# The first pair of ff tiles of a SwiGLU FFN as plain block products, with the sums of the seven-product scheme made behind them

## Chip, cores and metric

One Trainium2 chip, one core. The metric is device time of the whole program in microseconds (us), the median over runs of the same kernel. All data is float32. An operand of TensorE is a pair of reduced-precision float32 tiles, hi and lo (h is the rounded value, l what is left of it), and every product of two operands takes three matmuls: h·h, h·l and l·h.

## What is computed

Two layers over 640 tokens (128 of a prompt, 512 latent tokens), D = 1024. Layer 0 mixes tokens by attention and a state-space scan, layer 1 by a pooling mixer; each ends in a SwiGLU FFN with 22 ff tiles of 128. The part that the change touches is this:

```python
def swiglu(h, w_gate, w_up, w_down):
    return (jax.nn.silu(h @ w_gate) * (h @ w_up)) @ w_down

for l in range(DEPTH):
    ...                      # mix: MLA + SSD (layer 0), pool mixer (layer 1)
    xp = xp + g_p * rmsnorm(mix_p, norm_post_mix[l])
    xs = xs + g_s * rmsnorm(mix_s, norm_post_mix[l])
    fp = swiglu(modulate(xp, norm_pre_ffn[l], shf_p, scf_p), ffn_w_gate[l], ffn_w_up[l], ffn_w_down[l])
    fs = swiglu(modulate(xs, norm_pre_ffn[l], shf_s, scf_s), ffn_w_gate[l], ffn_w_up[l], ffn_w_down[l])
    xp = xp + gf_p * rmsnorm(fp, norm_post_ffn[l])
    xs = xs + gf_s * rmsnorm(fs, norm_post_ffn[l])
```

## The kernel before

**Tiles and halves.** Five token tiles of 128 hold the activations. For gate and up the 640 tokens are two halves of 320 (`HB`): half 0 is tokens 0 to 319, half 1 tokens 320 to 639. D is eight chunks of 128, four in each half of D. `prenorm` (L309 to L339) norms a token tile (square sum L315, root L104, reciprocal L105, scale L318 or L320 into `junk`), transposes it on TensorE (L328) into PSUM, and ACT (L335) and DVE (L333) evict it into `full`. The residual that is normed comes from L362, on DVE. Then `Halves.take(tt)` splits it.

**Seven products instead of eight.** The 22 ff tiles of gate and up are taken as 11 pairs. A `Matrix` is one pair of gate or of up, a 2 x 2 block matrix (ff tile x half of D), and so are the activations (half of D x half of the tokens). The four result blocks come from seven block products instead of eight, with sums of blocks on both sides; each product is 12 matmuls of 128x320 (four chunks, three each), at L497. So a pair needs 84 matmuls for each matrix, where plain products need 96. On the weight side `adds` (L467 to L470, POOL) makes the sums `q` and `t4` and overwrites a part of `rb`; `a`, `c`, `b` and `d` split raw weights or sums into hi (ACT, L89) and lo (L90, DVE unless another engine is named). On the activation side, `a1` holds the plain half 0, and `a2` five blocks on the columns of half 1: S2, S1, S3, S4 (sums) and A22 (plain). Products 1 and 2 use `a1` only; 6, 5, 7, 4 and 3 use `a2`.

**Where the sums are made.** For tiles 0 to 2 `take` splits into `a1` (DVE, L419 and L420). For tiles 3 and 4 it calls `pair`: three adds on DVE (L433, L435, L436), one on POOL (L434), into the tile `st`, then the splits into `a2h` (ACT, L410) and `a2l` (L411; DVE for the sums, POOL for A22).

**The order.** A scheduler of the framework sets the order of each engine's queue from the program's order, and each engine works through its queue in order. At an FFN's start, the first two tails (transposes and `take` of tiles 3 and 4) run among products 1 and 2 of the first gate g0 and the first up u0. Then, in the loop, product 6 and those after it follow. `p1`, `p2` and so on (L528 to L561) issue a product and what follows it: copies and adds of PSUM parts into `sg`, silu on ACT (L523), the gate's product with up on DVE (L526). `out_split` (L564 to L569) splits the gated tile into ah (ACT, L567) and al (POOL, L568); `down_add` multiplies it with w_down (L97 to L99, through `mm3`) and adds into `y` (L590), one pair later, in the slots `d()` between products. Raw weights come through a ring of four DMA buffers (`raw`), so a load waits until the work on an earlier one is done.

Of the kernel before, what the change touches and what calls it, by code (L numbers as in the profile page):

```python
# [9 lines left out]
F32 = mybir.dt.float32  # L10
# [7 lines left out]
P = 128  # L18
# [372 lines left out]
class Halves:  # L391
# [21 lines left out]
    def take(self, tt):  # L413
        nc = self.net.nc
        if tt < 3:
            cs = slice(tt * P, min(tt * P + P, HB))
            h, l = (a[:, :, cs] for a in self.a1)
            x = self.f[:, :, cs]
            nc.vector.tensor_copy(h, x)  # L419
            nc.vector.tensor_tensor(l, x, h.bitcast(F32), ALU.subtract)  # L420
        if tt == 3:
            self.pair(0, 64)
        if tt >= 3:
            self.pair(tt * P - HB, P)

    def pair(self, c0, n):
        nc = self.net.nc
        cs = slice(c0, c0 + n)
        fa, fb = self.f[:, :, cs], self.f[:, :, HB + c0 : HB + c0 + n]
        t = self.tmp.tile([P, 4, 4, P], F32, tag="st", name=self.net.name("st"))[:, :, :, 0:n]  # L430
        h, l = self.a2
        s1, s2 = t[:, self.S1], t[:, self.S2]
        nc.vector.tensor_tensor(s1, fb[:, 0:4], fb[:, 4:8], ALU.add)  # L433
        nc.gpsimd.tensor_tensor(t[:, self.S3], fa[:, 0:4], fb[:, 0:4], ALU.subtract)  # L434
        nc.vector.tensor_tensor(s2, s1, fa[:, 0:4], ALU.subtract)  # L435
        nc.vector.tensor_tensor(t[:, self.S4], fa[:, 4:8], s2, ALU.subtract)  # L436
# [63 lines left out]
def _ffn(net, l, A, fr, sp, tails, switch, finish):  # L500
# [112 lines left out]
    seq = [m for p in range(NPAIR) for m in mats(p)]
    seq[0], seq[1] = g0, u0
    prev = None
    wdn = None
    last = {}
    for n, m in enumerate(seq):
        p, up = divmod(n, 2)
        w = (wg, wu)[n] if n < 2 else Work(m, wg if up else None)  # L620
        if not up:
            wg = w
        nx = seq[n + 1] if n + 1 < len(seq) else None
# [3 lines left out]
        fill = [] if prev is None or final else list(range(NT))  # L627
# [16 lines left out]
        if nx and n != 0:  # L644
            nx.a()
# [13 lines left out]
        if up:  # L659
            at.append(out_split(wg, 1))  # L660
# [667 lines left out]
def trunk(ctx: ExitStack, tc: tile.TileContext, t: dict, o: dict):  # L1328
# [125 lines left out]
    A = Halves(net, ctx.enter_context(pool("a1", "right")))  # L1454

# [285 lines left out]
```

## Time and profile before

| | |
|---|---|
| median of 3 runs | 1479.79 us (1478.52 to 1483.55) |
| profiled execution | 1481.71 us |
| its span in the trace | 1479.9 us, mean granted clock 0.966 |
| PE busy | 1353.1 us, 91% |
| DVE busy | 1041.8 us, 70% |
| ACT busy | 662.5 us, 45% |
| POOL busy | 479.5 us, 32% |
| DMA | 164.38 MB, mean 111 GB/s |

PE is TensorE (its matmuls), DVE VectorE, ACT ScalarE, POOL GpSimd. A row of the timeline is: start in us from the start of the span, us that the work took, engine, line, operation, out<-in, shape, count, and in brackets the idle time of the engine just ahead of it with what ended that. Matmuls overlap, so the cost of one is the distance between two starts and not its own duration. [...]

### The profile page before, as it was taken

What the parts mean: (1) busy time and instruction counts of PE and PEld (TensorE: products, weight loads), DVE (VectorE), ACT (ScalarE), POOL (GpSimd) and SP (SyncE); (2) the same over time, 40 slices, a digit from 0 to 9 for tenths busy, and PEclk for the clock granted to TensorE, in tenths of its full rate; (3) what the DMA queues carried; (4) which work ended last, traced back from release to release, by engine and by line L of the source; (5) the groups of instructions that cost most, each with busy time, mean ns of one, the idle gap of its engine ahead of it and who ended that gap; (6) DMA issues with size and microseconds to landing.
All of it is one profiled execution on the core that took longest, in us unless ns stands there. A gap on an engine that the chain in (4) does not pass through costs nothing. (4 is left out here: it accounts for less than half of the span.)

```text
span 1479.9 us, 20167 instructions
## 1 busy us (share of the span) xinstructions
PE 1353.1 (91%) x7728; PEld 1152.2 (78%) x7728; DVE 1041.8 (70%) x1502; ACT 662.5 (45%) x1173; POOL 479.5 (32%) x385
## 2 busy tenths in 40 slices
PE   5999999999997599999999999855899999999997
PEld 2788764667576489898989998644789899999996
DVE  3755547787737777979876666898678766666656
ACT  3545645744225544343334334578353333433443
POOL 0000044244303553444253333322452533333320
PEclk8999999999998799999999999978899999999999
DMA  9434345500163232433332223221232332222213
GB/s 364 132 123 131 128 153 191 187 29 1 44 222 106 65 114 86 137 106 115 121 129 86 85 86 110 104 71 71 89 122 90 114 115 86 85 86 78 80 58 142
DMA packets 49988, 164.38 MB, mean 111 GB/s; under 512 B 6034, under 2 KB 9618, under 8 KB 49892
## 3 DMA queue, kind: packets, MB, share of 16 engines
q1 hardware_dynamic: 43056, 153.96, 31.4%
q10 hardware_dynamic: 6836, 9.14, 2.0%
q8 instruction: 60, 0.98, 0.3%
q14 instruction: 36, 0.29, 0.1%
HBM read 154.52 MB, written 8.56 MB: 110 GB/s over the span
## 5 line engine op out<-in xcount | busy, mean ns | idle before, releaser
L467 POOL TENSOR_TENSOR q<-raw,raw 128x512 f32<-128x512 f32 x44 | 62.8, 1427 | 451.5 <-DVE lc L90 225.8
L99 PE MATMUL ps<-hw,al 128*128 128x512 f32 x380 | 150.3, 396 | 4.4 <-POOL al L568 4.4
L590 DVE TENSOR_TENSOR y<-y,ps 128x512 f32<-128x512 f32 x180 | 120.5, 680 | 47.0 <-PE ps L99 46.3
L98 PE MATMUL ps<-lw,ah 128*128 128x512 f32 x380 | 150.4, 396 | 1.2 <-DVE lw L90 1.2
L97 PE MATMUL ps<-hw,ah 128*128 128x512 f32 x380 | 150.7, 396 | 0.0
L497 PE MATMUL ps<-a2h,hc 128*128 128x320 f32 x352 | 112.2, 320 | 38.0 <-ACT a2h L410 28.6
L497 PE MATMUL ps<-a2l,hc 128*128 128x320 f32 x352 | 112.0, 318 | 2.6 <-DVE a2l L411 2.6
L497 PE MATMUL ps<-a2h,lc 128*128 128x320 f32 x352 | 111.8, 319 | 0.0
L568 POOL TENSOR_TENSOR al<-sg,ah 128x640 fp32r<-128x640 f32 x44 | 82.4, 1877 | 90.8 <-ACT ah L567 69.4
L497 PE MATMUL ps<-a2h,lb 128*128 128x320 f32 x352 | 109.3, 311 | 0.0
L497 PE MATMUL ps<-a1h,ha 128*128 128x320 f32 x336 | 104.9, 312 | 4.9 <-DVE a1h L419 4.9
L497 PE MATMUL ps<-a2h,hb 128*128 128x320 f32 x352 | 109.0, 310 | 0.0
L497 PE MATMUL ps<-a2l,hb 128*128 128x320 f32 x352 | 108.8, 309 | 0.0
L497 PE MATMUL ps<-a1l,ha 128*128 128x320 f32 x336 | 104.5, 311 | 2.6 <-DVE a1l L420 2.6
L497 PE MATMUL ps<-a1h,la 128*128 128x320 f32 x336 | 104.3, 310 | 0.0
L497 PEld LDWEIGHTS ps<-a2h,hc 128*128 128x128 f32 x352 | 68.7, 196 | 41.3 <-ACT a2h L410 29.1
L90 DVE TENSOR_TENSOR lc<-q,hc 128x1024 fp32r<-128x1024 f32 x42 | 53.0, 1261 | 67.1 <-ACT hc L89 67.1
L99 PEld LDWEIGHTS ps<-hw,al 128*128 128x128 f32 x380 | 72.0, 190 | 23.4 <-POOL al L568 7.0
L89 ACT ACTIVATE hc<-q 128x1024 fp32r<-128x1024 f32 x44 | 46.6, 1059 | 94.6 <-PE ps L497 81.8
L98 PEld LDWEIGHTS ps<-lw,ah 128*128 128x128 f32 x380 | 72.2, 190 | 11.7 <-DVE lw L90 1.5
L97 PEld LDWEIGHTS ps<-hw,ah 128*128 128x128 f32 x380 | 72.1, 190 | 10.2
L89 ACT ACTIVATE hb<-raw 128x1024 fp32r<-128x1024 f32 x46 | 48.7, 1059 | 63.7 <-PE ps L497 31.6
(393 smaller groups left out, 3932.9 us busy)
## 6 DMA issues: line engine op xcount, KB each, us to landing
raw<-in_w_mod SPq DMA_DIRECT2D x80, 512.0 KB
raw<-in_w_gate SPq DMA_DIRECT2D x44, 512.0 KB
raw<-in_w_up SPq DMA_DIRECT2D x44, 512.0 KB
raw<-in_w_down SPq DMA_DIRECT2D x44, 512.0 KB
mraw<-in_w_mod SPq DMA_DIRECT2D x16, 512.0 KB
xs<-xd SPq DMA_DIRECT2D x10, 512.0 KB
x<-in_x_sample SPq DMA_DIRECT2D x8, 512.0 KB
raw<-in_w_xbc SPq DMA_DIRECT2D x8, 512.0 KB
```

The source lines that it names most:

```text
L89: self.nc.scalar.activation(h, x, AF.Copy)
L90: (eng or self.nc.vector).tensor_tensor(l, x, h.bitcast(F32), ALU.subtract)
L97: mm(out, ah, bh, start=first and i == 0, stop=False)
L98: mm(out, ah, bl, start=False, stop=False)
L99: mm(out, al, bh, start=False, stop=last and i == n - 1)
L467: g.tensor_tensor(self.q[:, lo], self.rb[:, lo], self.ra[:, lo], ALU.subtract)
L497: mm(out, x[:, k], z[:, k], start=first and n == 0, stop=n == len(terms) - 1, skip_group_check=True)
L568: nc.gpsimd.tensor_tensor(al, g.s[:, f], ah.bitcast(F32), ALU.subtract)
L590: nc.vector.tensor_tensor(yd, yd, out, ALU.add)
```

## The change

For the first pair of each FFN, gate and up are computed by plain block products. `plain(m, f, half)` makes one result block, 128 ff x 320 tokens, from eight chunks, so 24 matmuls through `mm3` (L97 to L99); silu reads PSUM, and the multiplication with up reads PSUM too (L626 and L628 of the kernel after). Half 1 needs plain activations: `take` now splits tiles 3 and 4 plainly, lower half of D into the slot S4 of `a2`, upper half into A22. The sums S1, S2 and S3 are made by `pair` behind the first half-1 product in the program; S4, whose slot is in use, is put into a spare part of `y` and split later by `fourth`. The weights of the first pair are split without sums, all four lo parts on POOL. `out_split` of the first pair is issued earlier, `gates` ahead of the loop, and the last pair's second al goes to DVE. PE's queue has 7011 rows instead of 6963.

```diff
@@ class Halves @@
+    def spare(self, y):
+        self.s4 = y.rearrange("p t d -> p (t d)")[:, NT * D - 4 * HB :].rearrange("p (k c) -> p k c", k=4)
+
+    def fourth(self):
+        h, l = self.a2
+        self.split(h[:, self.S4], l[:, self.S4], self.s4, self.net.nc.vector)
...
     def take(self, tt):
...
-        if tt == 3:
-            self.pair(0, 64)
-        if tt >= 3:
-            self.pair(tt * P - HB, P)
+        for c0, n in ((0, 64),) * (tt == 3) + ((tt * P - HB, P),) * (tt >= 3):
+            cs = slice(c0, c0 + n)
+            fb = self.f[:, :, HB + c0 : HB + c0 + n]
+            h, l = self.a2
+            for i, k in ((self.S4, 0), (self.A22, 4)):
+                self.split(h[:, i, :, cs], l[:, i, :, cs], fb[:, k : k + 4], nc.vector)
 
     def pair(self, c0, n):
...
-        nc.vector.tensor_tensor(t[:, self.S4], fa[:, 4:8], s2, ALU.subtract)
-        for i in range(2):
-            b = slice(2 * i, 2 * i + 2)
+        nc.vector.tensor_tensor(self.s4[:, :, cs], fa[:, 4:8], s2, ALU.subtract)
+        for b in (slice(0, 2), slice(2, 3)):
             self.split(
...
-        self.split(h[:, self.A22, :, cs], l[:, self.A22, :, cs], fb[:, 4:8], nc.gpsimd)
+
+    def plain(self, half):
+        if half == 0:
+            return [tuple(x[:, k] for x in self.a1) for k in range(KC)]
+        return [tuple(x[:, i, k] for x in self.a2) for i in (self.S4, self.A22) for k in range(4)]
@@ _ffn @@
-    def out_split(g, f):
+    def out_split(g, f, eng=None):
...
-        nc.gpsimd.tensor_tensor(al, g.s[:, f], ah.bitcast(F32), ALU.subtract)
+        (eng or nc.gpsimd).tensor_tensor(al, g.s[:, f], ah.bitcast(F32), ALU.subtract)
...
     g0, u0 = mats(0)
-    u0.tag_a = "w"
     g0.load()
     u0.load()
-    for m in (g0, u0):
-        m.a(nc.gpsimd)
-    g0.adds()
-    g0.c(nc.gpsimd)
-    wg = Work(g0)
-    wu = Work(u0, wg)
-    wg.p1()
+    w0 = {}
+    for f in range(2):
+        for m, tags in ((g0, "ab"), (u0, "cw")):
+            w0[m, f] = net.split(fr, tags[f], (m.ra, m.rb)[f], nc.gpsimd)
+    s0 = sp.tile([P, 2, TOK], F32, tag="sg", name=net.name("sg"))
+
+    def plain(m, f, half):
+        out = net.pt([P, HB])
+        wh, wl = (x.rearrange("p (k n) -> p k n", k=KC) for x in w0[m, f])
+        net.mm3(out, [(wh[:, k], wl[:, k], bh, bl) for k, (bh, bl) in enumerate(A.plain(half))])
+        d = s0[:, f, half * HB : half * HB + HB]
+        if m is g0:
+            nc.scalar.activation(d, out, AF.Silu)
+        else:
+            nc.vector.tensor_tensor(d, d, out, ALU.mult)
+
+    plain(g0, 0, 0)
     tails.pop(0)()
-    wg.p2()
-    wu.p1()
+    plain(u0, 0, 0)
     tails.pop(0)()
-    wu.p2()
+    plain(g0, 1, 0)
+    plain(u0, 1, 0)
+    plain(g0, 0, 1)
+    A.pair(0, 64)
+    A.pair(64, P)
+    plain(u0, 0, 1)
+    A.pair(192, P)
     switch(env)
     net.mrp = env["mac"]
-    g0.b()
-    g0.d()
...
+    seq = [m for p in range(1, NPAIR) for m in mats(p)]
+    n1 = seq[0]
+    n1.load()
+    at0 = [out_split(Out(s0), 0)]
+    n1.a()
+    n1.adds()
+    plain(g0, 1, 1)
+    n1.c()
+    plain(u0, 1, 1)
+    at0.append(out_split(Out(s0), 1))
+    n1.b()
+    n1.d()
+    A.fourth()
...
-            at.append(out_split(wg, 1))
+            at.append(out_split(wg, 1, nc.vector if final else None))
```

The order of the instructions shows what became of this. PE at the end of half 0 of the first FFN, before (`ps` is a PSUM tile, hw and lw the parts of u0's first operand, hc and lc those of the sum q of g0):

```order
L497 MATMUL ps_4604<-a1h,hw_4476 128x320
L497 MATMUL ps_4604<-a1l,hw_4476 128x320
L497 MATMUL ps_4604<-a1h,lw_4477 128x320
L497 MATMUL ps_4492<-a2h_4462,hc_4486 128x320
L497 MATMUL ps_4649<-a2h_4462,hc_4486 128x320
L497 MATMUL ps_4492<-a2l_4463,hc_4486 128x320
```

And after, at the same place (hw and lw are here the second ff tile of u0, ha and la the first of g0):

```order
L97 MATMUL ps_4615<-a1h,hw_4484 128x320
L98 MATMUL ps_4615<-a1l,hw_4484 128x320
L99 MATMUL ps_4615<-a1h,lw_4485 128x320
L97 MATMUL ps_4641<-a2h_4462,ha_4472 128x320
L98 MATMUL ps_4641<-a2l_4463,ha_4472 128x320
L99 MATMUL ps_4641<-a2h_4462,la_4473 128x320
```

The first matmuls on `a2` read sums S2 and S1 before, and plain activations in slot S4 after.

POOL at the start of the first FFN, before:

```order
L467 TENSOR_TENSOR q_4480<-raw_4466,raw_4464 128x512
L468 TENSOR_TENSOR q_4480<-raw_4466,q_4480 128x512
L469 TENSOR_TENSOR raw_4466<-raw_4466 128x512
L470 TENSOR_TENSOR t_891_4481<-raw_4464,q_4480 128x512
L90 TENSOR_TENSOR la_4473<-raw_4464,ha_4472 128x1024
L90 TENSOR_TENSOR lw_4477<-raw_4468,hw_4476 128x1024
L90 TENSOR_TENSOR lc_4487<-q_4480,hc_4486 128x1024
L411 TENSOR_TENSOR a2l_4463<-full_3857,a2h_4462 128x4x64
```

And after, where lines 446 and 482 to 485 are what lines 434 and 467 to 470 were:

```order
L90 TENSOR_TENSOR la_4473<-raw_4464,ha_4472 128x1024
L90 TENSOR_TENSOR lc_4477<-raw_4468,hc_4476 128x1024
L90 TENSOR_TENSOR lb_4481<-raw_4466,hb_4480 128x1024
L90 TENSOR_TENSOR lw_4485<-raw_4470,hw_4484 128x1024
L446 TENSOR_TENSOR st_4667<-full_3857 128x4x64
L482 TENSOR_TENSOR q_4741<-raw_4731,raw_4729 128x512
L483 TENSOR_TENSOR q_4741<-raw_4731,q_4741 128x512
L484 TENSOR_TENSOR raw_4731<-raw_4731 128x512
L485 TENSOR_TENSOR t_915_4742<-raw_4729,q_4741 128x512
```

The four adds ahead of la are gone, four weight splits stand in a row, and the next adds are those of the second gate.

ACT at the start of the second FFN, before (`sd` is the root of a square sum, of the table for square roots; `dump` is a square sum of the mix's output):

```order
L104 ACTIVATE sd_9098<-ss_1652_9090 128x1
L318 ACTIVATE junk_9051<-xs_8389,r_9055 128x1024
L531 ACTIVATE sg_9155<-ps_9157 128x320
L315 ACTIVATE junk_9105,ss_9106<-xs_8389 128x1024
L335 ACTIVATE full_8730<-ps_9171,mv_1571,mv_1572 128x128
L104 ACTIVATE sd_9108<-ss_9106,eps 128x1
L335 ACTIVATE full_8730<-ps_9171,mv_1571,mv_1572 128x128
L318 ACTIVATE junk_9105<-xs_8389,r_9109 128x1024
```

And after:

```order
L104 ACTIVATE sd_9093<-ss_1641_9085 128x1
L626 ACT_TABLE_LOAD
L626 ACTIVATE sg_9148<-ps_9149 128x320
L315 ACTIVATE junk_9100,ss_9101<-xs_8384 128x1024
L335 ACTIVATE full_8725<-ps_9175,mv_1571,mv_1572 128x128
L104 ACT_TABLE_LOAD
L104 ACTIVATE sd_9103<-ss_9101,eps 128x1
L335 ACTIVATE full_8725<-ps_9175,mv_1571,mv_1572 128x128 x2
L318 ACTIVATE junk_9100<-xs_8384,r_9104 128x1024
```

Where a copy stood (L531), silu stands, with a table load ahead of it and one ahead of the root that follows; a third load follows later, where before the only one was.

## Rows read from the trace of the kernel before

**Rows 1.** PE's waits, whole span: who waited for whom, us in total, times, longest.

```profile
PE ps L497 <- ACT a2h L410: 28.6, 2, 16.2
PE ps L497 <- DVE a2l L411: 2.6, 2, 2.3
```

**Rows 2.** Timeline of PE in the first FFN.

```profile
476.14 0.48 PE L328 MATMUL ps<-cm,junk 128*128 128x128 f32 x1 [2.19 <-DVE junk L320]
...
478.96 0.64 PE L497 MATMUL ps<-a1l,ha 128*128 128x320 f32 x1 [2.34 <-DVE a1l L420]
...
488.20 1.09 PE L328 MATMUL ps<-cm,junk 128*128 128x128 f32 x8 [0.84 <-DVE junk L320]
...
490.60 0.31 PE L497 MATMUL ps<-a1l,hw 128*128 128x320 f32 x1
490.75 0.31 PE L497 MATMUL ps<-a1h,lw 128*128 128x320 f32 x1
507.25 0.90 PE L497 MATMUL ps<-a2h,hc 128*128 128x320 f32 x2 [16.19 <-ACT a2h L410]
...
511.08 0.33 PE L497 MATMUL ps<-a2l,hc 128*128 128x320 f32 x1
```

**Rows 3.** Timeline of PE in the second FFN.

```profile
1016.24 0.33 PE L328 MATMUL ps<-cm,junk 128*128 128x128 f32 x1 [0.53 <-ACT junk L318]
...
1023.18 0.31 PE L497 MATMUL ps<-a1h,lw 128*128 128x320 f32 x1
1035.91 0.90 PE L497 MATMUL ps<-a2h,hc 128*128 128x320 f32 x2 [12.42 <-ACT a2h L410]
1039.10 0.63 PE L497 MATMUL ps<-a2l,hc 128*128 128x320 f32 x1 [2.29 <-DVE a2l L411]
1039.53 0.47 PE L497 MATMUL ps<-a2h,lc 128*128 128x320 f32 x1
...
1043.53 0.34 PE L497 MATMUL ps<-a2h,hc 128*128 128x320 f32 x1
...
1069.49 0.50 PE L99 MATMUL ps<-hw,al 128*128 128x512 f32 x1 [1.52 <-POOL al L568]
```

**Rows 4.** Windows: PE, PEld, DVE, ACT, POOL busy (x), PEclk, DMA share, GB/s.

```profile
500.00:510.00 10.00, 2.39 (x7) 1.99 (x8) 9.09 (x9) 3.06 (x3) 2.12 (x2) 0.50 0.18 52
```

**Rows 5.** Timeline of ACT and DVE in the first FFN's gap.

```profile
506.14 2.00 ACT L410 ACTIVATE a2h<-st 128x1024 fp32r<-128x1024 f32 x2 [4.68 <-DVE st L435]
...
500.23 1.21 DVE L411 TENSOR_TENSOR a2l<-st,a2h 128x1024 fp32r<-128x1024 f32 x1
```

**Rows 6.** Timeline of POOL and DVE at the first FFN's start.

```profile
473.02 2.51 POOL L90 TENSOR_TENSOR la<-raw,ha 128x1024 fp32r<-128x1024 f32 x1
475.48 2.88 POOL L90 TENSOR_TENSOR lw<-raw,hw 128x1024 fp32r<-128x1024 f32 x1
...
473.22 2.86 DVE L320 TENSOR_SCALAR junk<-x,r 128x1024 f32<-128x1024 f32 x1
476.01 2.90 DVE L420 TENSOR_TENSOR a1l<-full,a1h 128x512 fp32r<-128x512 f32 x1
```

**Rows 7.** Timeline of DVE and POOL in the pool mix.

```profile
959.30 4.95 DVE L362 SCALAR_TENSOR_TENSOR xs<-junk,r,xs 128x512 f32<-128x512 f32 x2
...
981.76 1.41 DVE L362 SCALAR_TENSOR_TENSOR xs<-junk,r,xs 128x512 f32<-128x512 f32 x2
...
985.21 1.78 POOL L467 TENSOR_TENSOR q<-raw,raw 128x512 f32<-128x512 f32 x1 [13.79 <-DMA raw<-in_w_up]
```

**Rows 8.** Timeline of ACT at its table load in the second FFN.

```profile
1023.79 1.28 ACT L523 ACT_TABLE_LOAD   x1
1025.08 0.47 ACT L523 ACTIVATE sg<-sg 128x320 f32<-128x320 f32 x1
```

**Rows 9.** Timeline of PE among the last products of the second FFN.

```profile
1448.86 0.50 PE L99 MATMUL ps<-ha,al 128*128 128x512 f32 x1 [0.80 <-POOL al L568]
```

More of the change, by code (lines that the diff above doesn't have):

```diff
@@ L429, in pair @@
         fa, fb = self.f[:, :, cs], self.f[:, :, HB + c0 : HB + c0 + n]
-        t = self.tmp.tile([P, 4, 4, P], F32, tag="st", name=self.net.name("st"))[:, :, :, 0:n]
+        t = self.tmp.tile([P, 3, 4, P], F32, tag="st", name=self.net.name("st"))[:, :, :, 0:n]
         h, l = self.a2
@@ L562, in p3, with __init__ @@
                 nc.vector.tensor_tensor(self.g.s[:, 1], self.g.s[:, 1], self.s[:, 1], ALU.mult)
-    def out_split(g, f):
+    class Out:
+        def __init__(self, s):
+            self.s = s
+    def out_split(g, f, eng=None):
         ah = env["at"].tile([P, TOK], F32R, tag="ah", name=net.name("ah"))
@@ L592, in _ffn @@
     g0, u0 = mats(0)
-    u0.tag_a = "w"
     g0.load()
     u0.load()
-    for m in (g0, u0):
-        m.a(nc.gpsimd)
-    g0.adds()
-    g0.c(nc.gpsimd)
-    wg = Work(g0)
-    wu = Work(u0, wg)
-    wg.p1()
+    w0 = {}
[13 more added lines that the diff above has]
+    plain(g0, 0, 0)
     tails.pop(0)()
-    wg.p2()
-    wu.p1()
+    plain(u0, 0, 0)
     tails.pop(0)()
-    wu.p2()
+    plain(g0, 1, 0)
[5 more added lines that the diff above has]
+    A.pair(192, P)
     switch(env)
     net.mrp = env["mac"]
-    g0.b()
-    g0.d()
[L613 to L616, printed above, removed]
+    seq = [m for p in range(1, NPAIR) for m in mats(p)]
[11 more added lines that the diff above has]
+    A.fourth()
+    prev = at0
+    wdn = net.split(fr, "w", down_load(0, 0), None)
+    env["gates"]()
     last = {}
-    for n, m in enumerate(seq):
+    for n, m in enumerate(seq, 2):
         p, up = divmod(n, 2)
-        w = (wg, wu)[n] if n < 2 else Work(m, wg if up else None)
+        w = Work(m, wg if up else None)
         if not up:
             wg = w
-        nx = seq[n + 1] if n + 1 < len(seq) else None
+        nx = seq[n - 1] if n - 1 < len(seq) else None
         final = p == NPAIR - 1
@@ L626, in _ffn @@
             last[0, 0] = net.split(fr, "w", down_load(NPAIR - 2, 0), None)
-        fill = [] if prev is None or final else list(range(NT))
+        fill = [] if final else list(range(NT))
         def d():
@@ L632, in d @@
             net.bg()
-        if nx and n != 0:
+        if nx:
             nx.load()
-        if n >= 2:
-            w.p1()
-            w.p2()
+        w.p1()
+        w.p2()
         if final and up:
@@ L643, in _ffn @@
         w.p5()
-        if nx and n != 0:
+        if nx:
             nx.a()
@@ L670, in _ffn @@
             prev = at
-        if nx and 1 <= n and (n + 1) // 2 < NPAIR - 1:
+        if nx and (n + 1) // 2 < NPAIR - 1:
             wdn = net.split(fr, "w", down_load((n + 1) // 2 - 1, (n + 1) % 2), None)
-        if n == 1:
-            env["gates"]()
     net.bg_drain()
@@ L1454, in trunk @@
     A = Halves(net, ctx.enter_context(pool("a1", "right")))
+    A.spare(y)
     def work_pools():
```

## The prediction

> **What bounds the kernel now.** The profiled execution took 1481.7 us over a span of 1479.9 us; the median of the three runs is 1479.8 us, so the profile lies 1.9 us above it. I make the sum as a difference and take it from both. A change of under 0.3% (4.4 us) is what a measurement of this kernel can't tell from none.
>
> I read the page first: TensorE (PE) is busy for 91% of the span, no other engine for more than 70%. So time comes back where PE waits, or where it does fewer matmuls. The list of what PE waits for shows where: the largest entry by far is two waits at L497 for a2h, 28.6 us together, one in each FFN; a2l adds 2.6 us to them [rows 1]. The timeline of PE gives each its place. In the first FFN half 0 ends with the matmul at 490.75, and the first matmul on a second-half operand starts at 507.25, after 16.19 us [rows 2]. In the second FFN the same gap is 12.42 us, with 2.29 us more for a2l [rows 3]. [...] What DVE and ScalarE (ACT) do there is build five blocks for tokens 320 to 639 from the last token tile and split each into hi and lo.
>
> **What the change removes.** The first pair of ff tiles no longer needs the sums. Half 1 of it reads the plain second-half activations, which `take` splits as soon as a tile's transposes are evicted. After the change the first matmul of half 1 needs a 128x512 split of the last tile, not three adds and two 128x1024 splits behind them. Does a matmul wait for its own block or for all of tile a2h? In the row of ACT at 506.14 two ACTIVATEs to a2h fill 2.00 us, to 508.14 [rows 5], while PE had started at 507.25 [rows 2]: the wait is for the block. So the sums can follow behind.
>
> Is PE busy long enough until they are there? Half 1 is now 4 x 24 = 96 matmuls, and products 1 and 2 of the next gate, which need only half 0, are 24 more. The spacing of full-clock matmuls is 0.147 us (0.15 from 490.60 to 490.75 [rows 2]), so they take 17.6 us. Tile 4 is transposed ahead of the last two plain products of half 0, another 7.1 us, from which I take 2 off for evicting it. DVE's queue from the last tile's split to the last split of S1 and S2 holds, by the order, eleven instructions on 512 columns (0.70 each, half of the 1.41 for two [rows 7]), four on 1024 (1.21 [rows 5]) and a multiply or two: 13 to 14 us. GpSimd (POOL), with its own `st` subtractions, may hold DVE back by up to some 3.5 us, as much as DVE lost at 959.30 [rows 7]. That is 17 us of work under 22 us of cover, so I count the a2h wait as gone in both layers, with little to spare.
>
> **First FFN.**
> - a2h, and this layer's 0.3 of a2l (2.6 less the 2.29 of the other): -16.2 - 0.3 = -16.5 us [rows 1 to 3].
> - The matmuls behind that wait run at 0.27 us each until 511.08 [rows 2], some ten of them; without the gap they don't: 10 x 0.12 = -1.2 us.
> - The start. POOL's four adds ended where la began, at 473.02, and la, lw and lc followed. DVE's scale of tile 3 at 473.22 took 2.86 us, as long as la kept POOL, and a1l at 476.01 took 2.90, as long as lw did [rows 6]. PE waited for both, 2.19 and 2.34 us [rows 2]. In the new order no adds stand ahead of la; la still can't start before ha is split, about when it starts now, but DVE, no longer slowed by the adds, should have the scale done by then, and a1l ends behind POOL's first split instead of its second: about 476 instead of 478.9, -3.0 us; 0 if the scale comes a moment late.
> - The last tile's transposes, which waited 0.84 us at 488.20 [rows 2]. PE comes to them 2 us earlier (the start, less twelve more matmuls ahead of them); the DVE passes that they wait for are each held by one POOL split, and move up by one split too: -0.8 us, bounds -0.8 and +2.
> - 24 more matmuls in each layer than the seven products need (4 x 48 = 192 instead of 2 x 84 = 168): 24 x 0.147 = +3.5 us.
> - The first matmul of half 1 may wait for the last tile's own a2l: +0.9 us, one 128x512 split of 0.70 and some queueing. Bounds 0 and 4.
>
> Sum -17.1 us, from -12.5 (start no earlier, a2l somewhat late) to -21 (a2l in time, and pair 1's waits for al gone as well, which I leave as they are, since POOL's adds for the next up stand ahead of the second al).
>
> The four weight splits now go to POOL one after the other, lb among them. What the rows show of DVE beside such a split is above: 2.86 and 2.90 us, where POOL's took 2.51 and 2.88 [rows 6]. [...]
>
> **Second FFN.**
> - a2h and a2l: -12.4 - 2.3 = -14.7 us [rows 3].
> - Seventeen matmuls at the lower clock, up to 1043.53 (fifteen spacings of 0.267 from 1039.53 on): 17 x 0.12 = -2.0 us [rows 3].
> - The wait of tile 3's transposes, 0.53 [rows 3]: -0.5 us.
> - The wait for al at 1069.49, 1.52 us [rows 3]: al of the first pair is now made well ahead of pair 1's down products, and here no add for a later up stands ahead of it: -1.5 us.
> - 24 more matmuls: +3.5 us.
> - A new wait. Silu of the first gate now comes between the square roots of the last tiles: ACT gets two more table loads, 1.28 each [rows 8], and the reciprocal for tile 4 stands on DVE behind the multiply with the first up product, which PE finishes just ahead of tile 4's transposes. What is then late is that multiply, the reciprocal and one ACT pass over 128x1024 (1.0, half of the 2.00 for two [rows 5]); I estimate +2.2 us. Bounds 0 and 5 (both loads on the chain too).
>
> Sum -13.0 us, from -9 to -15.
>
> By the row the ACTIVATE after a load starts as the load ends, at 1025.08 [rows 8]. [...]
>
> **The pool mix ahead of the second FFN.** Its DVE chain is what PE waits for there, and the new POOL splits and the reordered hd and ld of the next gate fall into it. DVE's pair at L362 took 4.95 us beside a POOL split and 1.41 alone [rows 7]. One more split costs DVE about 2.2 us (3.5 at most), ld of 0.70 comes in and lb of 1.21 goes to POOL: +1.7 us, bounds -0.5 and +4.5. hd on ACT now waits, in the middle of that chain, for POOL's last add, which waits for a weight load; that is rival two.
>
> **The end.** The last al goes from POOL to DVE; PE's wait for it was 0.80 us [rows 9]: -0.8, bounds -0.8 and 0. Silu straight from PSUM and the fewer copies are off PE's path; the matmuls that hide them run for longer than they do, and they count nothing.
>
> **Sum:** -17.1 - 13.0 + 1.7 - 0.8 = -29.2 us: 1481.7 to 1452.5 in a profile, 1479.8 to 1450.6 at the median. With all bounds on one side: -37.3 and -17.0, or 1442.5 to 1462.8.
>
> **The rivals.**
> 1. *The wait comes back smaller.* The sums, or the last tile's own splits, are late: ACT does a part of the last tile's split behind hd, hd waits for POOL's adds, and those for a raw tile whose buffer comes free only when POOL has split the matrix in it. For it: work and cover are only 5 us apart. Against: the raw tiles are the first two that come free. Six us in a layer: 1456.6 if in one, 1462.6 if in both.
> 2. *The pool mix pays.* The whole stage shifts by a load-and-add chain, 8 us instead of 1.7: 1456.9. For it: POOL waited there 13.79 us for a raw tile ahead of its adds at 985.21 [rows 7]. Against: the list of PE's waits has no entry of any size for these adds, so the chain there has room for them so far.
> 3. *Slower than before: TensorE stays at its lower level through the plain products.* In both layers it ran so behind the gap [rows 2, 3, 4]. Price: (2 x 192 - 27) matmuls x 0.12 = +43 us, 1493; from some 243 matmuls at that level (29.2 / 0.12) the gain is gone. For it: the plain products begin where PE has just waited. Against: the lower level ended within some seventeen matmuls each time.
> 4. *The change doesn't do what it says:* half 1 waits for the whole a2 tile, sums included. Of the waits of 16.5 and 14.7 us the longer half 0 covers 7 in each layer, and 17 us stay: 1468. Against it stands the row of 506.14 [rows 5].
>
> **How the numbers follow.** Forecast 0.72, rival one 0.15, rival two 0.07, rival three 0.04, rival four 0.02. The predicted time is the forecast's, 1450.6. Its bounds, 1442.5 to 1462.8, hold rivals one and two as well; I give 1442 to 1463 for eight in ten. Faster by over 0.3% are the forecast and rivals one, two and four, 0.96, less 0.02 for mishaps that add up; slower is rival three, 0.04; within 0.3% is the 0.02 left.
>
> **What would show it.** Right: no PE wait for a2h over 3 us; the 192 plain matmuls of a layer joined in some 30 us with two or three short waits, granted clock 1.0 in most of it; a1l of the first FFN ending behind la; a wait of 2 us ahead of tile 4's transposes in the second FFN, with three table loads there. Wrong: a wait of 4 us or more at the first half-1 matmul or at product 6 of pair 1 (rival one), the second FFN starting much later after its pool mix began (rival two), clock 0.5 through the plain stretch (rival three).

## The result, and the profile after

The changed kernel takes 1455.87 us at the median (1451.67 to 1460.46) where the kernel before takes 1480.3; the ratio is 0.9833 with a 95% interval of 0.9804 to 0.9863, so 24.4 us less (20 to 29 by the ratio). Measured once more as `again`, it gives 0.9835 (0.9815 to 0.9856). The forecast was 29.2 us less, 1450.6. Profile against profile it is 1455.05 against 1481.71, 26.7 us less.

What PE waited for in the kernel after (who waits for whom, us in total, times, longest):

```profile
PE ps L328 <- ACT junk L318: 16.3, 3, 8.9
PE ps L512 <- ACT sg L546: 16.3, 5, 5.2
PE ps L328 <- DVE junk L320: 12.6, 2, 8.2
...
PE ps L98 <- DVE a2l L419: 0.7, 1, 0.7
```

The 28.6 us for a2h [rows 1] are off the list, and 0.7 for a2l is what is left. At its head now stand, level with a wait of the transposes (L328), the waits for sg of L546: the copy of product 1, which product 6 waits for, since product 6 adds into the PSUM tile that this copy reads (L512 is the old L497). The timeline of PE tells where, first in the first FFN:

```profile
474.64 0.63 PE L97 MATMUL ps<-a1h,ha 128*128 128x320 f32 x1 [3.65 <-ACT ha L89]
477.49 0.63 PE L99 MATMUL ps<-a1h,la 128*128 128x320 f32 x1 [1.61 <-POOL la L90]
...
496.79 0.41 PE L98 MATMUL ps<-a2l,ha 128*128 128x320 f32 x1 [0.69 <-DVE a2l L419]
...
519.52 0.64 PE L512 MATMUL ps<-a2h,hc 128*128 128x320 f32 x1 [5.01 <-ACT sg L546]
...
522.35 0.47 PE L512 MATMUL ps<-a2l,hc 128*128 128x320 f32 x1
522.62 0.47 PE L512 MATMUL ps<-a2h,lc 128*128 128x320 f32 x1
```

then in the second:

```profile
1007.51 1.09 PE L328 MATMUL ps<-cm,junk 128*128 128x128 f32 x8 [2.19 <-ACT junk L318]
...
1038.47 0.64 PE L512 MATMUL ps<-a2h,hc 128*128 128x320 f32 x1 [5.24 <-ACT sg L546]
...
1083.52 0.50 PE L99 MATMUL ps<-hw,al 128*128 128x512 f32 x1 [0.93 <-POOL al L587]
```

Two of the same waits in the kernel before, for product 6 and for al, first and second FFN:

```profile
532.96 0.41 PE L497 MATMUL ps<-a2h,hc 128*128 128x320 f32 x1 [1.69 <-ACT sg L531]
537.92 0.50 PE L99 MATMUL ps<-hw,al 128*128 128x512 f32 x1 [1.51 <-POOL al L568]
...
1064.53 0.41 PE L497 MATMUL ps<-a2h,hc 128*128 128x320 f32 x1 [1.83 <-ACT sg L531]
...
1109.58 0.50 PE L99 MATMUL ps<-hw,al 128*128 128x512 f32 x1 [1.19 <-POOL al L568]
```

Where 16.19 and 12.42 us were [rows 2, 3], half 1 starts after 0.69 us and without a wait. But product 6 of pair 1, which waited 1.69 and 1.83 us in the kernel before, waits 5.01 and 5.24 us, and the matmuls behind it stand 0.27 us apart, where those of the plain products stand 0.15 apart. The waits for the first pair's al, 5 us behind product 6, are gone in both FFNs (1.51 at 537.92 and 1.52 at 1069.49 [rows 3]). The 0.93 at 1083.52, 45 us behind product 6, is for the al of pair 1 and stood at 1109.58 with 1.19.

Windows of the changed kernel (length, busy time of PE, PEld, DVE, ACT, POOL with counts, granted clock as a share of full speed, DMA share, GB/s):

```profile
500.00:505.00 5.00, 5.00 (x36) 5.00 (x36) 4.18 (x6) 1.69 (x2) 0.22 (x2) 1.00 0.00 0
...
520.00:525.00 5.00, 5.00 (x17) 4.21 (x16) 5.00 (x5) 0.88 (x2) 5.00 (x4) 0.54 0.35 108
```

The plain products run at full clock (1.00, beside 0.50 in the old gap [rows 4]); behind the wait at product 6 the clock is 0.54.

All kernels by stage, from PE's and DVE's timelines. "First FFN" goes from its first matmul on a1h to the wait for al among its last products, "between" from there to the first matmul on a1h of the second FFN, "second FFN" from there to the last L362:

| kernel | ratio to before, 95% interval | first FFN, us | between | second FFN |
|---|---|---|---|---|
| before | 1 | 451.7 | 87.9 | 462.3 |
| changed | 0.9833 (0.9804 to 0.9863) | 435.1 | 87.3 | 451.5 |
| again | 0.9835 (0.9815 to 0.9856) | 437.1 | 88.8 | 451.4 |
| layer0_only | 0.9905 (0.9888 to 0.9922) | 436.6 | 87.4 | 460.7 |
| sums_early | 0.9840 (0.9810 to 0.9870) | 436.9 | 85.1 | 450.7 |
| copy_first | 0.9862 (0.9840 to 0.9885) | 437.8 | 87.4 | 451.8 |
| less_dve | 0.9889 (0.9869 to 0.9909) | 443.8 | 87.7 | 454.2 |
| less_pool | 0.9786 (0.9761 to 0.9811) | 433.4 | 85.7 | 448.9 |
| order3 | 0.9824 (0.9807 to 0.9840) | 437.1 | 85.8 | 452.5 |
| order3_silu | 0.9839 (0.9822 to 0.9857) | 436.7 | 85.2 | 450.1 |
| gates_late | 0.9866 (0.9850 to 0.9882) | 436.3 | 88.9 | 452.8 |
| order3_gates | 0.9757 (0.9744 to 0.9771) | 434.6 | 87.5 | 446.0 |
| order3_gates_silu | 0.9751 (0.9730 to 0.9771) | 431.9 | 87.1 | 446.3 |
| lo_on_vector | 0.9771 (0.9753 to 0.9790) | 436.6 | 85.6 | 449.6 |

A stage of one profile is good to about 2 us: `again` is the changed kernel. Ahead of the first FFN, where no kernel differs, its start lies between 469.2 and 476.4 us.

### The profile page after: what moved, and what is told of

Its sections match the earlier page's. It is cut to its first block, busy times and chain, and to the rows that moved or that the text cites. A ratio compares the mean times of both kernels' runs of the same rounds, so it can differ in the third digit from the quotient of the medians.

```text
span 1453.0 us, 20201 instructions
## 1 busy us (share of the span) xinstructions
PE 1355.7 (93%) x7776; PEld 1159.2 (80%) x7776; DVE 1031.3 (71%) x1498; ACT 656.7 (45%) x1165; POOL 450.2 (31%) x363
## 4 chain that ended last, share of the span: by engine, by line
PE 43%; DVE 10%; issue 5%; POOL 4%; ACT 3%; DMA 1%; POOLq 0%; DVEq 0%; ACTq 0%
PE ps L512 25%; PE ps L99 6%; PE ps L97 5%; PE ps L98 5%; DVE macc L275 3%; POOL al L587 1%; DVE y L609 1%; DVE a2l L419 1%; PE ps L1653 1%; DVE lc L90 1%; POOL t L485 1%; POOL q L483 1%; DMA raw<-in_w_mod 1%; POOL q L482 1%; ACT full L335 1%
## 5 line engine op out<-in xcount | busy, mean ns | idle before, releaser
L99 PE MATMUL ps<-hw,al 128*128 128x512 f32 x380 | 150.0, 395 | 1.2 <-POOL al L587 1.2
L97 PE MATMUL ps<-hw,ah 128*128 128x512 f32 x380 | 150.6, 396 | 0.0
L512 PE MATMUL ps<-a2h,hc 128*128 128x320 f32 x320 | 101.0, 316 | 16.3 <-ACT sg L546 16.3
L512 PE MATMUL ps<-a2h,lc 128*128 128x320 f32 x320 | 100.8, 315 | 0.0
L512 PE MATMUL ps<-a2l,hc 128*128 128x320 f32 x320 | 100.6, 314 | 0.0
L512 PE MATMUL ps<-a2h,lb 128*128 128x320 f32 x320 | 99.2, 310 | 0.0
L512 PE MATMUL ps<-a2h,hb 128*128 128x320 f32 x320 | 98.9, 309 | 0.0
L512 PE MATMUL ps<-a2l,hb 128*128 128x320 f32 x320 | 98.8, 309 | 0.0
L512 PE MATMUL ps<-a1h,la 128*128 128x320 f32 x320 | 98.8, 309 | 0.0
L512 PE MATMUL ps<-a1h,ha 128*128 128x320 f32 x320 | 98.7, 308 | 0.0
L512 PE MATMUL ps<-a1l,ha 128*128 128x320 f32 x320 | 98.7, 308 | 0.0
L99 PEld LDWEIGHTS ps<-hw,al 128*128 128x128 f32 x380 | 71.8, 189 | 19.0 <-POOL al L587 2.6
L98 PEld LDWEIGHTS ps<-lw,ah 128*128 128x128 f32 x380 | 72.2, 190 | 11.7 <-DVE lw L90 1.6
L97 PEld LDWEIGHTS ps<-hw,ah 128*128 128x128 f32 x380 | 72.2, 190 | 10.3
L275 DVE SCALAR_TENSOR_TENSOR macc<-raw,silc,macc 128x512 f32<-128x512 f32 x84 | 75.4, 935 | 4.5 <-DMA raw<-in_w_mod 4.5
L512 PEld LDWEIGHTS ps<-a2h,hc 128*128 128x128 f32 x320 | 61.4, 192 | 19.1 <-ACT sg L546 17.6
```

Of the source, the lines that this page charges most:

```text
L97: mm(out, ah, bh, start=first and i == 0, stop=False)
L98: mm(out, ah, bl, start=False, stop=False)
L99: mm(out, al, bh, start=False, stop=last and i == n - 1)
L275: nc.vector.scalar_tensor_tensor(acc[:, v], x[:, k2 * 512 : k2 * 512 + 512], self.silc[:, kc, v : v + 1], acc[:, v] if kc else bb, op0=ALU ...
L512: mm(out, x[:, k], z[:, k], start=first and n == 0, stop=n == len(terms) - 1, skip_group_check=True)
```

## The experiments

**Each layer's share.** `again` is the changed kernel. `layer0_only` has the change in the first FFN; the second calls the old functions.

```diff
-        return _ffn(net, l, A, fr, sp, lag, switch, fin)
+        A.old = l != 0
+        return (_ffn_old if A.old else _ffn)(net, l, A, fr, sp, lag, switch, fin)
```

> The changed kernel once more, in more rounds, as the measure for the others of this call. Theory one (the sum of the prediction, less the longer wait at product 6): 24 to 27 us below the kernel before, ratio 0.982 to 0.984. Rival (the first four runs were favourable or unfavourable by their spread of 9 us): anywhere from 0.980 to 0.986. The waits of PE at product 6 of pair 1 should be 5.0 and 5.2 us again if they come from the order of the queues, and differ by more than 1 us if they come from chance.

> The change in the first FFN alone; the second FFN and the pool mix ahead of it are those of the kernel before. Theory one (each layer's gain is its own): 16 to 18 us below the kernel before, the second FFN with its waits of 12.4 and 2.3 us for a2h and a2l as before. Rival (the layers have equal shares, half of the whole): 12 to 13 us. Rival (what the trace shows as the first layer's gain is given back at its end, in the stores and loads that follow): under 8 us.

`again` agrees with the first measurement, though the wait at product 6 of the first FFN came out as 3.43 instead of 5.01 us, with 2.10 instead of 0.69 at half 1: the sum is the same, the place moves. By the mark set ahead of the run (more than 1 us of difference), that wait is in part chance; the second FFN's 5.24 came again. The first layer alone brings 0.95% (0.78 to 1.12), 14 us (11.5 to 16.6), and so the second some 10. Nothing is given back, but between equal shares and 16 to 18 us the interval doesn't decide; by the stages above, the layers' shares are 15 and some 10 us. The old second FFN has its wait of 12.4 us.

**Where the sums stand.** `sums_early` makes each tile's sums right behind its plain split:

```diff
             for i, k in ((self.S4, 0), (self.A22, 4)):
                 self.split(h[:, i, :, cs], l[:, i, :, cs], fb[:, k : k + 4], nc.vector)
+            self.pair(c0, n)
...
-    A.pair(0, 64)
-    A.pair(64, P)
     plain(u0, 0, 1)
-    A.pair(192, P)
```

> The changed kernel with the sums made right behind the plain split of each token tile, ahead of the plain products of half 1 in the program, instead of behind the first of them; the plain products stay. Theory one (half 1 waits only for the plain split of the last tile; the sums of tile 3 ahead of it on VectorE delay it): 2 to 5 us more than the changed kernel, a new wait of 2 to 5 us at the first matmul of half 1 in each layer. Rival (the gain comes from where the sums stand and not from the plain operands): the waits of 12 to 16 us are back, 15 to 25 us more than the changed kernel. Rival (the sums are in nobody's way): the same within 1 us.

New waits came, as theory one had them, though not of its size in the first FFN. PE in the first FFN of `sums_early`:

```profile
498.47 0.41 PE L97 MATMUL ps<-a2h,ha 128*128 128x320 f32 x1 [2.43 <-ACT a2h L418]
...
502.63 0.64 PE L98 MATMUL ps<-a2l,ha 128*128 128x320 f32 x1 [3.61 <-DVE a2l L419]
```

In the second FFN it is 2.12 us. The time did not grow: 0.9840, the same as the changed kernel's. The 6.0 us at the start of half 1 are paid back at product 6, which no longer waits. So what the sums' place in the program decides is only on which side of half 1 the wait lies. The gain is the plain operands', not that of the sums "made behind".

**Why product 6 waits.** Three engines' rows of the changed kernel, first FFN (ACT, then DVE, then POOL):

```profile
518.41 0.74 ACT L586 ACTIVATE ah<-sg 128x640 fp32r<-128x640 f32 x1 [2.73 <-DVE sg L628]
519.05 0.42 ACT L546 ACTIVATE sg<-ps 128x320 f32<-128x320 f32 x1
...
513.28 2.18 DVE L90 TENSOR_TENSOR lb<-raw,hb 128x1024 fp32r<-128x1024 f32 x1 [0.35 <-ACT hb L89]
515.39 2.59 DVE L419 TENSOR_TENSOR a2l<-y,a2h 128x1280 fp32r<-128x1280 f32 x1
517.90 0.47 DVE L628 TENSOR_TENSOR sg<-sg,ps 128x320 f32<-128x320 f32 x1
...
512.38 2.00 POOL L587 TENSOR_TENSOR al<-sg,ah 128x640 fp32r<-128x640 f32 x1 [2.33 <-ACT ah L586]
514.33 2.29 POOL L482 TENSOR_TENSOR q<-raw,raw 128x512 f32<-128x512 f32 x1
```

The copy of product 1 (L546) is ready to go and stands on ACT behind the second `ah`. That waits for the last multiply with up (L628), which stands on DVE behind a split for the next gate (lb) and the late split of S4. Both took longer than such a split did elsewhere: lb 2.18 us beside POOL's first al (the other two splits of that gate took 1.22 and 1.23), and S4's 2.59 beside the first of POOL's adds for the second up (1.48 in `less_pool` below, where these adds are left out). In the second FFN there is one more in the row, a DMA issue of the gates' background work on ACT, which waits for a memset on POOL:

```profile
1037.98 0.44 ACT L546 ACTIVATE sg<-ps 128x320 f32<-128x320 f32 x1 [1.03 <-POOL bb L265]
```

`copy_first` issues the copy ahead of both, by an order edge (`issue_after`), which sets the place in the engine's queue and waits for nothing:

```diff
-    at0.append(out_split(Out(s0), 1))
...
-    env["gates"]()
...
         w.p1()
+        if n == 2:
+            cp = net.nc.cur_bb.bb.instructions[-1]
+            with net.tc.issue_after(cp):
+                at0.append(out_split(Out(s0), 1))
+                env["gates"]()
         w.p2()
```

(the same edge stands ahead of the background work in pair 1).

> The changed kernel with one order edge: on ScalarE the copy of product 1 of the second gate is issued ahead of the second ah of the first pair and ahead of the DMA issues of the gates. Theory one (product 6 waits 5.0 and 5.2 us because that copy stands in ScalarE's queue behind ah, which waits for a multiply on VectorE, and behind a DMA issue that waits for GpSimd): both waits fall to 0.5 to 2 us, the lower clock behind them goes, 5 to 10 us are gained over the changed kernel. Rival (the operand S2 of product 6 is itself late, the sums being made too late): the wait stays at 4 to 5 us with another releaser, a2h or a2l, and the time is that of the changed kernel within 1 us.

The waits at product 6 fell to 1.01 and 2.35 us and still end with the copy, so S2 was there: the rival falls. There is no room to spare in the second FFN, though: in the changed kernel S2's last split ends at 1033.56, 0.3 us after PE is free for product 6 (1038.47 less 5.24). The gain did not come, 0.9862, which is the changed kernel's time within the intervals. PE in the first FFN of `copy_first`:

```profile
512.98 0.41 PE L512 MATMUL ps<-a2h,hc 128*128 128x320 f32 x1 [1.01 <-ACT sg L546]
...
516.86 0.50 PE L98 MATMUL ps<-lw,ah 128*128 128x512 f32 x1 [1.62 <-DVE lw L90]
...
522.14 0.80 PE L99 MATMUL ps<-hw,al 128*128 128x512 f32 x1 [4.09 <-POOL al L587]
```

Two waits took its place: for the lo part of the down weights, and for the second al, which stands on POOL behind the four adds.

**Less work for one engine.** Two kernels leave work out, to see which engine is short: `less_dve` the three lo splits of the second gate, `less_pool` the adds for the second up.

```diff
-    n1.a()
+    n1.wa = net.hi(fr, "a", n1.ra), w0[u0, 1][1]
...
-    n1.c()
+    n1.wc = net.hi(fr, "c", n1.q), w0[u0, 1][1]
...
-    n1.b()
+    n1.wb = net.hi(fr, "b", n1.rb), w0[u0, 1][1]
```

```diff
-        if nx:
+        if nx and n == 2:
+            nx.q, nx.t4 = m.q, m.t4
+        elif nx:
             nx.adds()
```

> The changed kernel with work left out: the lo parts la, lc and lb of the second gate's weights are not computed on VectorE, a tile of the first pair's lo parts stands in for them (the products of that gate are wrong by their lo terms). Theory two (behind half 1 VectorE has more to do than the cover of 22 us holds; the wait at product 6 and the waits that took its place when the copy was moved are all its lateness): three splits of 1.2 to 2.2 us less, the 5.0 and 5.2 us at product 6 fall to about 1 to 2 us and no other wait takes their place, 5 to 9 us below the changed kernel. Rival (GpSimd's adds for the second up are the bound, and hold al): the wait goes over to al at the down product, under 2 us gained.

> The changed kernel with other work left out: GpSimd's four adds for the second up are not done, the second gate's sums stand in for them (that up is wrong). Theory two (VectorE's own work is what is late): only what the adds held VectorE back by comes out, 2 to 3 us in each layer at product 6, so 3 to 6 us below the changed kernel. Rival (GpSimd is the bound): product 6 keeps a wait of 3 us or more from the order of ScalarE's queue, but al is early, the down product waits for nothing, and the gain is under 2 us on this base, since al was not waited for here either.

`less_dve` came out 8 us slower than the changed kernel, which neither theory had. Rows of DVE, then of ACT, in its first FFN:

```profile
513.74 1.80 DVE L424 TENSOR_TENSOR a2l<-y,a2h 128x1280 fp32r<-128x1280 f32 x1 [4.96 <-ACT a2h L423]
515.47 0.47 DVE L633 TENSOR_TENSOR sg<-sg,ps 128x320 f32<-128x320 f32 x1
...
532.37 1.22 DVE L90 TENSOR_TENSOR lw<-raw,hw 128x1024 fp32r<-128x1024 f32 x1
...
522.87 1.06 ACT L89 ACTIVATE ha<-raw 128x1024 fp32r<-128x1024 f32 x1 [5.84 <-POOL bb L270]
```

DVE is idle for 4.96 us, and product 6 still waits 3.59 (5.59 in the second FFN): the multiply stands behind the S4 split all the same, which waits for ACT. ACT's next weight split stands behind a DMA issue that waits for POOL's memset, 5.84 us. So at product 6 it isn't VectorE's load but what stands ahead in the queues. The time of `less_dve` shows nothing of that load, because the edit brings a wait of its own: the tile that stands in is lw of the first pair, its pool has one buffer for it, and the lo part of the down weights goes into the same buffer. So DVE makes that one only when the second gate's last matmul on the stand-in (530.97) is done, at 532.37; in the changed kernel it stands 14 us earlier:

```profile
518.30 1.89 DVE L90 TENSOR_TENSOR lw<-raw,hw 128x1024 fp32r<-128x1024 f32 x1
```

PE then waits for lw twice, 0.52 and 2.25 us, within 30 us of product 6, where the changed kernel has no such wait. How much of the 8 us this makes, beside the other order that the scheduler chose, isn't settled. `less_pool` gained 0.47% over the changed kernel, some 7 us, with 1 to 13 by the two intervals, so theory two's 3 to 6 is not excluded; product 6 of the second FFN waits 0.22 instead of 5.24 us, that of the first still 3.88. POOL's adds cost in two ways: they hold DVE (in the first FFN the S4 split takes 1.48 instead of 2.59 us without them and lw 1.21 instead of 1.89), and the memset that the DMA issue waits for stands behind them (in the second FFN the copy no longer waits for it).

**The order alone, and with the gates out of the way.** `order3` adds two more edges to `copy_first`: the second al ahead of the adds on POOL, lw ahead of the S4 split on DVE.

```diff
-    A.fourth()
...
     wdn = net.split(fr, "w", down_load(0, 0), None)
+    with net.tc.issue_after(net.nc.cur_bb.bb.instructions[-1]):
+        A.fourth()
...
                 at0.append(out_split(Out(s0), 1))
+                al2 = net.nc.cur_bb.bb.instructions[-1]
...
-        if nx:
+        if nx and n == 2:
+            with net.tc.issue_after(al2):
+                nx.adds()
+        elif nx:
             nx.adds()
```

> No work left out, three order edges on the changed kernel: on ScalarE the copy of product 1 ahead of the second ah and the gates' DMA issues; on GpSimd the second al ahead of the adds for the second up; on VectorE the lo part of the down weights ahead of the late S4 split. Theory two, with order as its half (each wait that took the place of the 5 us was a queue position: 4.1 us for al, 1.6 and 2.5 us for lw): the first FFN gets 4 to 5 us shorter than the changed kernel's, the second 2 to 3 us, 1448 to 1451. Rival (the work is the bound, whatever the order): another wait appears, at product 7, 4 or 3 of pair 1 or at the second gate's successors, and the time is that of the changed kernel within 2 us.

The waits for the first pair's al and for lw are gone, and once more others appear, as the rival had it. PE and ACT in the first FFN of `order3`:

```profile
515.53 0.41 PE L512 MATMUL ps<-a2h,hc 128*128 128x320 f32 x1 [1.01 <-ACT sg L546]
...
527.25 0.50 PE L512 MATMUL ps<-a2h,hd 128*128 128x320 f32 x1 [2.43 <-ACT sg L564]
...
526.47 0.25 ACTq L266 DMA_DIRECT2D bb<-in_b_mod  x1
526.76 0.44 ACT L564 ACTIVATE sg<-ps 128x320 f32<-128x320 f32 x1 [3.61 <-POOL bb L265]
```

The last two rows (ACTq is ACT's queue) name the next one: the copy at L564 stands behind the gates' DMA issue, which waits for the memset behind POOL's adds. `gates_late` moves `env["gates"]()` from ahead of the loop to the end of pair 1 (`if n == 3`), `order3_gates` does both.

> The changed kernel with the gates' background work (sixteen multiply-adds of 0.7 us on VectorE, memsets on GpSimd, DMA issues on ScalarE for the next modulation vectors) issued at the end of pair 1 instead of ahead of it; nothing else moves. Theory three (behind half 1 the queues are short of time for the next weights, and the gates take VectorE's time there): pair 1 loses 2 to 4 us of waits in each layer, and in the second FFN the 1.0 us that the copy of product 1 stands behind a memset goes from the 5.2 at product 6; 1449 to 1453. Rival (the wait at product 6 is only the order of ScalarE's queue, ah ahead of the copy): product 6 waits 3.4 to 5 us as before in the first FFN, and the time is that of the changed kernel within 2 us.

> The three order edges of order3 and the gates behind pair 1. Theory three (the order edges gave nothing since the wait went over to the sums for the second up, which GpSimd and VectorE make while the gates take their time): with both, the waits at product 6 (1.0 us), 5 and 4 (0.7 and 2.4 us in order3) all get smaller, 3 to 6 us below order3 and below the changed kernel: 1447 to 1451. Rival (GpSimd's adds alone are the bound): within 2 us of order3.

Alone, the move gives nothing: in `gates_late` product 6 waits 4.99 and 5.28 us. What moved, by the rows, are the multiply-adds (in the first FFN the first of them comes 87.1 us after the FFN's start instead of 45.5) and the second memset with its DMA issue. The first memset and its issue stayed where they were, and the copy in the second FFN still stands behind them:

```profile
1042.65 0.44 ACT L546 ACTIVATE sg<-ps 128x320 f32<-128x320 f32 x1 [1.03 <-POOL bb L265]
```

So the multiply-adds are not what makes product 6 wait; that 1.03 us of the DMA issue was not taken out by this run. It is even 0.3% above the changed kernel, at the edge of the intervals; the stages give 1 us here and there, and no row that I found explains it. Both together give 0.9757, 11 us below the changed kernel; in the second FFN, 446.0 instead of 451.5 us, PE then has no wait over 0.4 us in the first 100 us but that for tile 4; the 2.42 us that `order3` had there for the copy at L564 are gone. PE's busy time in the first 100 us of each FFN, in the changed kernel and in `order3_gates`:

```profile
474.64:574.64 100.00, 92.58 (x541) 87.07 (x542) 82.82 (x91) 50.15 (x81) 52.43 (x29) 0.92 0.33 103
997.04:1097.04 100.00, 91.64 (x555) 86.35 (x554) 72.57 (x87) 56.74 (x93) 34.45 (x20) 0.97 0.28 93
```

```profile
474.21:574.21 100.00, 95.80 (x576) 90.43 (x577) 77.89 (x89) 51.91 (x83) 50.95 (x30) 0.96 0.33 102
996.32:1096.32 100.00, 97.48 (x609) 92.35 (x608) 67.79 (x85) 57.66 (x95) 36.90 (x24) 1.00 0.30 98
```

35 and 54 more matmuls fit into the same 100 us, with the granted clock up from 0.92 to 0.96 and from 0.97 to 1.00.

**Silu put off.** A copy in place of the first silu, which then stands behind the last root:

```diff
-            nc.scalar.activation(d, out, AF.Silu)
+            nc.scalar.activation(d, out, AF.Copy if (f, half) == (0, 0) else AF.Silu)
         else:
+            if (f, half) == (0, 0):
+                nc.scalar.activation(d, d, AF.Silu)
             nc.vector.tensor_tensor(d, d, out, ALU.mult)
...
     tails.pop(0)()
-    plain(u0, 0, 0)
     tails.pop(0)()
+    plain(u0, 0, 0)
```

> As order3, and silu of the first gate block is put off behind the last square root, with a plain copy in its place, and the last tile's transposes are asked for ahead of the first up product. Theory one (the new wait of 2.19 us ahead of tile 4's transposes in the second FFN is made by the two table loads and by the multiply that the reciprocal stands behind): one table load instead of three, that wait falls to under 0.7 us, 1.5 to 2.5 us below order3. Rival (tile 4's chain of square sum, root and scale is itself the longer one): the wait stays at 2 us and the time is that of order3.

> order3_gates with silu of the first block put off as in order3_silu. In order3_silu the second FFN was 2.4 us shorter than in order3, though the wait ahead of tile 4's transposes did not fall. Theory: that comes again, 1 to 3 us below order3_gates. Rival (the 2.4 us were the lower clock in one profile): the same within 1 us.

The wait ahead of tile 4's transposes did not fall: 2.67 and 2.97 us instead of 2.19, and in the first FFN there is a new one of 2.03 and 2.13. But the edit does two things, and PE now comes to these transposes 24 matmuls (3.5 us) earlier, since the up product no longer stands ahead. The chain of tile 4 itself did get shorter. In the second FFN it runs from the end of the first gate product, which these rows of ACT follow (the changed kernel, then `order3_silu`):

```profile
1001.00 1.28 ACT L626 ACT_TABLE_LOAD   x1 [1.59 <-PE ps L99]
...
998.40 0.44 ACT L626 ACTIVATE sg<-ps 128x320 f32<-128x320 f32 x1 [1.61 <-PE ps L99]
```

The transposes start at 1007.51 and at 1001.84, so 6.5 us became 3.4: two loads of 1.28 and the multiply of 0.49 are out of it, as theory one had it. Had the up product stayed ahead, it would by these numbers have covered the 3.4 us (an estimate; that was not run). The times differ from the kernels without it by no more than the intervals (0.9839 and 0.9824; 0.9751 and 0.9757); the 2.4 us of one profile did not come again.

**Two of POOL's splits on DVE.** `lo_on_vector`:

```diff
-            w0[m, f] = net.split(fr, tags[f], (m.ra, m.rb)[f], nc.gpsimd)
+            w0[m, f] = net.split(fr, tags[f], (m.ra, m.rb)[f], nc.vector if f else nc.gpsimd)
```

> The changed kernel with the second ff tile's lo parts, lb and lw, made on VectorE instead of GpSimd. Theory one (POOL's four splits hold VectorE one instruction each): GpSimd holds VectorE for two splits only, but VectorE takes 2 x 1.21 us of its own; the last tile's square sum and scale come 2 to 3 us earlier, the time is within 2 us of the changed kernel. [...] Rival (VectorE has no room there): 3 us or more above it.

0.9771, some 9 us below the changed kernel, 4 to 14 by the two intervals: theory one with its 2 us falls, and so does the rival, 3 us or more above the changed kernel. Waits of PE in it:

```profile
PE ps L512 <- ACT sg L546: 15.2, 5, 4.8
PE ps L328 <- ACT junk L318: 14.6, 4, 5.0
PE ps L328 <- DVE junk L320: 9.1, 2, 5.9
```

The waits of the transposes (L328) come to 23.7 us; in the changed kernel they are 12.6 for DVE and 16.3 for ACT, 28.9; the 2.19 ahead of tile 4 is 1.07. What a POOL split did to DVE shows in the scale of tile 4 in the first FFN, in the changed kernel beside the split lw (on POOL for 2.58 us from 483.03), and in `lo_on_vector`, where DVE makes lw itself:

```profile
483.46 2.70 DVE L320 TENSOR_SCALAR junk<-x,r 128x1024 f32<-128x1024 f32 x1
...
481.01 0.75 DVE L320 TENSOR_SCALAR junk<-x,r 128x1024 f32<-128x1024 f32 x1
```

The 5 us of waits are not 5 us of time by stage: the stage between the FFNs is 1.7 us shorter than the changed kernel's and the second FFN 1.9, the first is 1.5 longer, all within the 2 us, and 2.5 us lie ahead of the first FFN, where nothing differs. So the gain stands on the times of the runs, and where it arises I can't say.

## Why the prediction was right, and where its sum was off

**The main mechanism was right.** Half 1 waits for the plain split alone (0.69 us, 2.10 in `again`, forecast 0.9), the matmul waits for its block and not for the tile (half 1 waits last at 496.79, while the last split of a sum into the same tile starts at 508.18), and the sums hide behind half 1. In the first 100 us of the FFNs PE was busy for these times in the kernel before:

```profile
473.45:573.45 100.00, 74.86 (x425) 69.21 (x426) 76.04 (x85) 48.37 (x76) 55.20 (x34) 0.85 0.28 87
1013.07:1113.07 100.00, 79.97 (x477) 73.78 (x476) 71.10 (x82) 55.13 (x92) 44.47 (x27) 0.91 0.31 100
```

and after for 92.58 and 91.64: 17.7 and 11.7 us less idle, 29.4. By the forecast's terms it was 16.5 + 3.0 + 0.8 - 0.9 = 19.4 and 14.7 + 0.5 + 1.5 - 2.2 = 14.5, 33.9. By stage, the first FFN came out 16.6 us shorter (14.6 in `again`) where the forecast had 17.1, and the second 10.8 (10.9) where it had 13.8 with the last al. That the first is so near is in part luck, since two errors in it offset each other, as the next paragraph shows.

**The mis-sized term is the cover behind half 1.** I counted the sums, 17 us, under 22 us of cover, and asked whether S2 is late. It isn't (`copy_first`). But in the same queues stand the splits of the next gate (three, of 1.2 to 2.2), the late S4 split (2.59), ah and al of the first pair, the adds for the second up and the gates; the sum has no term for a longer wait at product 6, and gives no reason for that. It went from 1.69 to 5.01 and from 1.83 to 5.24: +6.7 us. The forecast's own mark for this, 4 us or more at product 6 (rival one), did appear, in both layers and at about half of the price of 6, though with another cause than rival one's: not late operands, but a copy behind others in ACT's queue. Against it stand 1.5 us for al in pair 1 of the first FFN, which I had not counted as gone; the 1.52 of the second FFN went as forecast.

**The lower clock came back with it.** I took off 1.2 and 2.0 us for matmuls behind the old gap. Behind product 6's wait some twelve matmuls of 320 columns run at 0.27 us instead, and four of 512 columns at 0.43 instead of 0.23: by these spacings about 2 us in each FFN, so of the 3.2 us nothing is left.

**Right to within a microsecond:** tile 4's wait in the first FFN, 0.84, gone; the new one in the second, 2.19, forecast 2.2; the last al, 0.80, no longer waited for. The start of the first FFN is right in its number: 4.53 us of waits for the scale and for a1l became 1.61 for la, -2.9, forecast -3.0. It isn't in its mechanism. I had a1l end behind POOL's first split; it is done ahead of it, and PE waits for that split itself:

```profile
474.50 0.68 DVE L430 TENSOR_TENSOR a1l<-full,a1h 128x512 fp32r<-128x512 f32 x1
...
474.67 2.77 POOL L90 TENSOR_TENSOR la<-raw,ha 128x1024 fp32r<-128x1024 f32 x1 [64.19 <-ACT ha L89]
```

The table load stands between two ACTIVATEs here too, with 0.02 us on either side, so by the rows it cost ACT its own 1.28 us:

```profile
1003.66 0.45 ACT L335 ACTIVATE full<-ps,mv,mv 128x128 f32<-128x128 f32 x1
1004.13 1.28 ACT L104 ACT_TABLE_LOAD   x1
1005.43 0.29 ACT L104 ACTIVATE sd<-ss,eps 128x1 f32<-128x1 f32 x1
```

**The pool mix** was forecast at +1.7 and is 87.3 and 88.8 us long against 87.9, about nothing, within the bounds. One reading behind that term was wrong: DVE's pair of 4.95 us [rows 7] stood beside two POOL splits and not one, 2.64 us from 958.32 and 2.79 from 960.92, so by these rows a split cost it about 1.8 us, half of 4.95 less 1.41, where I took 2.2 (3.5 at most). The stage alone can't price the splits: kernels that leave it as it is spread over 85.1 to 88.9 us. That isn't to say that POOL's splits are cheap, since `lo_on_vector` gains more than I priced them at. The scale of tile 4, 2.70 us beside a split and 0.75 without one, and the 5 us of waits for the transposes (28.9 to 23.7) that go when DVE makes two of the four lo parts itself say the same.

**The rivals.** Three, TensorE at its lower level through the plain products, did not come (1.00 in the windows above), nor did four, the wait for the whole tile; two, the pool mix, neither.

The changed kernel can be bettered: with the order edges and the gates behind pair 1 it takes 0.9757 of the time before, about 36 us less, and with two lo parts on DVE 0.9771. The two were not tried together.

## What to carry to other kernels

When a wait is filled with other work, list everything that is queued on each engine in that stretch, and not only what the removed wait was for: the new critical wait here was a small copy standing in order behind instructions that nobody was in a hurry for. A reordering that moves one such wait moves the next into its place (copy, al, lw, DMA issue), so follow the row that ends each wait to its queue and mend all of them before judging by the time: one edge alone gave nothing or less, all with the gates 11 us. When work is left out as a test, look at which buffer the stand-in keeps: in `less_dve` that made a new wait.

## What the runs showed of the hardware that I had not expected

A DMA issue on ScalarE's queue that waited for another engine held up the compute behind it: behind one that waited for a 0.5 us memset on GpSimd, itself behind other work, ScalarE stood idle for 3.61 us ahead of a 0.4 us copy in `order3` and for 5.84 us ahead of a weight split in `less_dve`.
